# Moving tensor_tensor work from GpSimd to VectorE, deeper buffers in the first norm, and float32r parts for the modulation products

## The chip, the cores and the metric

The kernel runs on one core of a Trainium2 chip. The metric is the device time of one execution in microseconds (us). The median of three runs of the kernel before is 2357.48 us (2355.71 to 2359.46).

## The reference

One inference step of a two-layer hybrid diffusion model on 640 tokens: 512 latent tokens and 128 context tokens, D = 1024, all float32. Per layer:

```python
mod = silu(c) @ w_mod[l] + b_mod[l]          # 1024 -> 6*1024, for c and for c_ctx
sh1, sc1, g1, sh2, sc2, g2 = split(mod, 6)
h = rmsnorm(x, g_pre_mix) * (1 + sc1) + sh1
z = h @ w_in                                  # one projection for three mixers and the gates
oa, ob, oc = windowed_gqa(z), latent_attention(z), qknorm_gqa(z)
m = sum(sigmoid(gate_i) * (o_i @ w_oi)) @ w_out
x = x + g1 * rmsnorm(m, g_post_mix)
h = rmsnorm(x, g_pre_mlp) * (1 + sc2) + sh2
x = x + g2 * rmsnorm(square(relu(h @ w_mlp1)) @ w_mlp2, g_post_mlp)
```

The new keys and values of the context tokens are outputs too.

## The kernel before

**Products.** A float32 matrix product is made from float32r parts: each operand is split into a high part (ScalarE copies it into a float32r tile) and a low part (VectorE subtracts the high part from the source), and three products hi*hi, hi*lo, lo*hi are added up in PSUM (`mm3`, L574). `unit` (L540) loads a weight block into a `wr` buffer and splits it into `wh` and `wl`; these come from a ring of `NW` = 4 buffers. The modulation is the exception: there TensorE takes plain float32 operands.

**Stages.** `run` (L1913) goes through `first_norm` (RMSNorm of the five 128-token tiles, transposes, and the first two modulation vectors of layer 0), then per layer: `b_proj`, `b_rope`, `b_heads` (latent attention), the two GQA mixers in four groups (`gqa_group`), `merge`, `wout` with `post` and `norm_mod` after each token tile, `mlp1_first`, `sums` and 14 rounds of `mlp1_pair` (one Strassen-Winograd level: seven products for two column blocks of the MLP; the weights are first combined into s1 to s4), and `mlp2_block`. Gates (`gate_gen`) and modulation (`mod_gen`) are fillers: `drive` advances them at given rates while attention or MLP runs.

**Order.** All instructions are first recorded by `Recorder` (L168) and then ordered per engine by a list scheduler: `one` (L386) simulates engines with the costs of `cost`, `latest` (L361) computes the latest finishing time of each instruction, which becomes its rank on VectorE, ScalarE, GpSimd and SyncE in the next of 8 passes; the best pass is emitted (L528, so nearly all rows of the profile have line L528). In `one` a transfer holds the network for its bytes / 300e3 us. The scheduler also knows that a GpSimd tensor_tensor and a VectorE instruction with operands in SBUF alone lengthen each other.

**What the change touches.** `first_norm` (L823): the token tiles `x0` have 3 buffers, the 1 MB weight blocks `mw` 4 (`[P, 4, 512]`, eight blocks in all); a float32 matmul has the 128x2 condition vectors `scT` as its stationary operand and gives a 2x512 row, which ScalarE copies (`modrow`) and four small transposes turn into columns (`modt`). The first projection (`b_proj`, 288 columns) runs in two halves, k = 0 to 3 and k = 4 to 7, since the normed inputs `hh`/`hl` of k = 4 to 7 need the second half of these vectors. `mod_gen` (L715): two accumulators of 128x512, one for each condition vector, take eight weight rows per half vector; the first is accumulated by VectorE (`scalar_tensor_tensor`), the second by a ScalarE scaling and a GpSimd add. The sum over partitions is a float32 matmul against ones: for gates (v = 2, 5) 128x512 outputs, otherwise eight products with one column. GpSimd also adds in `rope` (called from `kv_evac`, `q_evac`, `b_rope`), in `prompt_group`, `merge`, `post` (token tiles 0 and 1) and `mlp1_pair` (s1 to s4, name `s` in the profile). Its normalisation of probabilities (`normalise`, L987, tile `pt`) and the `pow` of the norms (`rs`, `hrs`) are not touched.

Of the kernel before, what the change touches and what calls it, by code (L numbers as in the profile page):

```python
# [11 lines left out]
F32 = mybir.dt.float32  # L12
F32R = mybir.dt.float32r
# [4 lines left out]
P = 128  # L18
# [149 lines left out]
class Recorder:  # L168
# [192 lines left out]
    def latest(self, everything, end):  # L361
# [10 lines left out]
        for o in reversed(self.done):  # L372
            for p, data in o.preds.items():
                t = o.late
                if data:
                    t -= p.end - p.start
                    if o.eng is not None and p.eng != o.eng:
                        t -= self.LAT
# [7 lines left out]
    def one(self, everything, look):  # L386
# [49 lines left out]
        while True:  # L436
# [32 lines left out]
            if o.dma:  # L469
                net = max(net, t + 1.6) + wait / 300e3  # L470
# [61 lines left out]
class Step:  # L532
# [70 lines left out]
    def setup(self, ctx):  # L603
# [36 lines left out]
        self.scT = c.tile([P, 2, 8], F32, name="scT")  # L640
        self.modT = [c.tile([P, 6, 8, 2], F32, name=f"modT{l}") for l in range(DEPTH)]
# [23 lines left out]
    def cond(self):  # L665
# [9 lines left out]
        nc.vector.tensor_tensor(self.scT.rearrange("p s k -> p (s k)"), cT, r, ALU.mult)  # L675
        for l in range(DEPTH):
# [38 lines left out]
    def mod_gen(self, mp, l, vecs, own=0):  # L715
# [3 lines left out]
        for v in vecs:  # L719
            for hf in range(2):  # L720
                c0 = v * D + hf * 512
                acc = [mp.tile([P, 512], F32, name=f"macc{s}", tag=f"macc{s}", bufs=1) for s in range(2)]
                for u in range(4):
# [6 lines left out]
                    for j in range(2):  # L730
# [5 lines left out]
                        else:  # L736
                            nc.vector.scalar_tensor_tensor(out=acc[0], in0=rv[:, j, :], scalar=s0, in1=acc[0],
                                                           op0=ALU.mult, op1=ALU.add)
                            nc.scalar.activation(rv[:, j, :], rv[:, j, :], AF.Copy, scale=s1)
                            nc.gpsimd.tensor_tensor(acc[1], acc[1], rv[:, j, :], ALU.add)  # L740
                    yield
                isg = v in (2, 5)
                if isg:
# [5 lines left out]
                    for s in range(2):  # L749
                        ps = self.bank("mps", "pt")  # L750
                        nc.tensor.matmul(ps, self.ones, acc[s], start=True, stop=True)
# [4 lines left out]
                else:  # L756
                    ps = self.bank("mps", "pt")
                    pv = ps[:, :8].rearrange("p (n s) -> p n s", s=2)
                    for n in range(4):
                        for s in range(2):  # L760
                            nc.tensor.matmul(pv[:, n, s:s + 1], acc[s][:, n * P:n * P + P], self.ones[:, 0:1], start=True, stop=True)
# [61 lines left out]
    def first_norm(self, pool, xin):  # L823
# [3 lines left out]
        xs = [pool.tile([P, D], F32, name="x0", tag="x0", bufs=3) for t in range(NT)]  # L827
# [15 lines left out]
        for n in range(2):  # L843
            if n == 1:
                self.first = self.proj_units(I["w_in"][0], 768 + 384, 288, 3)
            for v in (1, 0):
                ps = self.lin_ps()
                for kh in range(2):
                    raw = pool.tile([P, 4, 512], F32, name="mw", tag="mw", bufs=4)
                    nc.sync.dma_start(raw, self.wsrc(w, 4 * kh, 4, v * D + n * 512, 512))  # L850
                    for i in range(4):
                        k = 4 * kh + i
                        nc.tensor.matmul(ps[:2, :], self.scT[:, :, k], raw[:, i], start=k == 0, stop=k == KC - 1)
                row = pool.tile([2, 512], F32, name="modrow", tag="modrow", bufs=2)
                nc.scalar.activation(row, ps[:2, :], AF.Copy)
                tps = self.bank("modt", "pt")
                pv = tps[:, :8].rearrange("p (n s) -> p n s", s=2)
# [1298 lines left out]
```

## Time and profile before

| | |
|---|---|
| median of 3 runs | 2357.48 us |
| profiled execution, its own time | 2356.36 us |
| its span | 2354.6 us |
| PE busy | 2286.6 us, 97% |
| PEld busy (weight loads, beside PE) | 2089.6 us, 89% |
| DVE (VectorE) busy | 1700.6 us, 72% |
| ACT (ScalarE) busy | 1289.2 us, 55% |
| POOL (GpSimd) busy | 763.2 us, 32% |
| DMA | 317.10 MB, 135 GB/s |

PE is TensorE. A matmul's record covers its pass through the array, so consecutive records overlap; what a matmul costs in a dense stretch is the distance from its start to the start of the next one. A float32 matmul shows as two records.

### The profile page before, as it was taken

Reading aid. Unit: us, or ns where it says so; the run is one execution under the profiler, and the core shown is the slowest. Engines: PE = TensorE matmul, PEld = TensorE weight load, DVE = VectorE, ACT = ScalarE, POOL = GpSimd, SP = SyncE. Lnnn points to the kernel's source line nnn. Section 1 sums busy time; section 2 is a strip of 40 time slices with the busy share of each in tenths; the row PEclk is TensorE's granted clock in tenths of the full one; section 3 lists DMA queues with packets and bytes.
Section 4 is the critical chain, followed back from the end, with each engine's and each line's share of the span. In section 5 each row is a group of like instructions: output and inputs, shape, how many; then the busy total and the mean of one; then the engine's idle time right before and its main releaser. Section 6 shows DMA issues by size and latency. Waiting matters only on the chain. (4 is left out here: it accounts for less than half of the span.)

```text
span 2354.6 us, 39546 instructions
## 1 busy us (share of the span) xinstructions
PE 2286.6 (97%) x14303; PEld 2089.6 (89%) x14303; DVE 1700.6 (72%) x3351; ACT 1289.2 (55%) x3000; POOL 763.2 (32%) x671
## 2 busy tenths in 40 slices
PE   8999999999999999999999999999999999999998
PEld 3988999989998999888889889899999889998886
DVE  3778488897675998867477866998846669884444
ACT  4577466676435565744265765767743356664222
POOL 1322044562132475223033212455412315650001
PEclk9999999999999999999999999999999999999999
DMA  7431244343663454664244222434346544446332
GB/s 252 112 91 50 86 121 129 104 107 96 218 208 113 149 170 146 224 209 150 80 134 113 65 82 75 127 105 125 109 152 187 177 135 150 165 139 215 117 120 81
DMA packets 252451, 317.10 MB, mean 135 GB/s; under 512 B 37328, under 2 KB 169696, under 8 KB 251744
## 3 DMA queue, kind: packets, MB, share of 16 engines
q1 hardware_dynamic: 252256, 314.58, 42.9%
q8 instruction: 113, 1.85, 0.3%
q14 instruction: 82, 0.67, 0.1%
HBM read 251.84 MB, written 57.44 MB: 131 GB/s over the span
## 5 line engine op out<-in xcount | busy, mean ns | idle before, releaser
L528 DVE TENSOR_TENSOR wl<-wr,wh 128x256 fp32r<-128x256 f32 (+5 forms) x772 | 370.5, 527 | 145.0 <-ACT wh L528 143.6
L528 ACT ACTIVATE wh<-wr 128x256 fp32r<-128x256 f32 (+5 forms) x772 | 276.2, 421 | 257.5 <-PE lps L528 140.0
L528 POOL TENSOR_SCALAR pt<-pt,rc 128x640 f32<-128x640 f32 (+1 forms) x192 | 167.4, 879 | 315.3 <-DVE rc L528 261.2
L528 PE MATMUL lps<-wh,ah 128*128 128x512 f32 x640 | 252.8, 395 | 0.0
L528 PE MATMUL lps<-wh,al 128*128 128x512 f32 x640 | 252.4, 394 | 0.0
L528 PE MATMUL lps<-wl,ah 128*128 128x512 f32 x640 | 251.9, 394 | 0.0
L528 POOL TENSOR_TENSOR rs<-ss,mhalf 128x1 f32<-128x1 f32 x60 | 37.1, 619 | 497.5 <-DVE ss L528 496.6
L528 DVE TENSOR_TENSOR pl<-tps,ph 128x512 fp32r<-128x512 f32 (+2 forms) x240 | 147.8, 631 | 30.3 <-ACT ph L528 27.6
L528 ACT ACTIVATE pt<-sps,nm 128x640 f32<-128x640 f32 (+2 forms) x192 | 141.7, 741 | 50.9 <-DVE nm L528 48.6
L528 PE MATMUL sps<-h2h,wl 128*128 128x320 f32 (+2 forms) x464 | 145.0, 313 | 9.8 <-DVE wl L528 9.8
L528 ACT ACTIVATE ph<-tps 128x512 fp32r<-128x512 f32 (+2 forms) x240 | 130.4, 555 | 33.0 <-PE tps L528 29.9
L528 PE MATMUL sps<-h2h,wh 128*128 128x320 f32 (+2 forms) x464 | 145.9, 314 | 0.0
L528 PE MATMUL tps<-ident,pt 128*128 128x128 f32 x896 | 140.5, 275 | 5.2 <-POOL pt L528 1.9
L528 PEld LDWEIGHTS lps<-wl,ah 128*128 128x128 f32 x640 | 120.1, 188 | 28.5 <-issue 0.2
L528 PEld LDWEIGHTS lps<-wh,ah 128*128 128x128 f32 x640 | 120.1, 188 | 28.0 <-issue 0.5
L528 PE MATMUL sps<-h2l,wh 128*128 128x320 f32 (+2 forms) x464 | 144.6, 312 | 0.0
L528 PEld LDWEIGHTS lps<-wh,al 128*128 128x128 f32 x640 | 120.1, 188 | 27.5
L528 POOL TENSOR_TENSOR macc<-macc,wr 128x512 f32<-128x512 f32 x84 | 118.3, 1409 | 57.2 <-ACT wr L528 44.4
L528 POOL TENSOR_TENSOR s<-wq 128x512 f32<-128x512 f32 x56 | 89.8, 1604 | 142.4 <-DMA wq<-in_w_mlp 116.9
L528 POOL TENSOR_TENSOR macc<-macc,mr 128x512 f32<-128x512 f32 x56 | 87.7, 1566 | 140.5 <-ACT mr L528 92.9
L528 DVE TENSOR_TENSOR wl<-s,wh 128x512 fp32r<-128x512 f32 x112 | 123.3, 1114 | 3.4 <-ACT wh L528 2.2
L528 PE MATMUL gps<-hh,wh 128*128 128x320 f32 x384 | 120.1, 313 | 2.2 <-ACT th L528 1.7
(335 smaller groups left out, 7371.4 us busy)
## 6 DMA issues: line engine op xcount, KB each, us to landing
wr<-in_w_in SPq DMA_DIRECT2D x72, 512.0 KB, 3.8
wr<-in_w_mlp SPq DMA_DIRECT2D x72, 512.0 KB, 4.0
wq<-in_w_mlp SPq DMA_DIRECT2D x56, 512.0 KB, 4.1
wr<-in_w_mod SPq DMA_DIRECT2D x48, 512.0 KB, 3.8
ar<-a SPq DMA_DIRECT2D x56, 320.0 KB, 4.5
mr<-in_w_mod SPq DMA_DIRECT2D x32, 512.0 KB, 4.6
th<-th SPq DMA_DIRECT2D x96, 160.0 KB, 1.9
tg<-th SPq DMA_DIRECT2D x48, 320.0 KB, 3.1
```

What stands on the lines that cost most here:

```text
L528: getattr(getattr(self.nc, o.eng), o.name)(*args, **kw)
```

## The change

Every GpSimd `tensor_tensor` over full tiles becomes a VectorE one; in `mod_gen` the scaling and the add become one VectorE `scalar_tensor_tensor`. Both accumulators are then split into float32r parts and multiplied with float32r ones, or with a 128x2 selector `pick` whose 2x512 result is copied and transposed as in the first norm. In `first_norm` the weights are split on chip into `wh`/`wl`, the condition vectors into four columns `scs` (two high, two low), so one float32 matmul becomes two float32r ones with four columns; `x0` has 5 buffers, `mw` 8, and the weights of the first projection are recorded after the norm instead of inside it. In the scheduler a transfer now counts as 370e3 bytes per us, and the latest time of what feeds a transfer's reader is taken from that.

```diff
@@ latest / one
-                    t -= p.end - p.start
+                    t -= 2.3 + p.wait / 370e3 if p.dma else p.end - p.start
-                net = max(net, t + 1.6) + wait / 300e3
+                net = max(net, t + 1.6) + wait / 370e3
@@ cond
+        for i in range(2):
+            nc.vector.tensor_copy(self.scs[:, :, i], self.scT[:, i, :])
+            nc.vector.tensor_tensor(self.scs[:, :, 2 + i], self.scT[:, i, :], self.scs[:, :, i].bitcast(F32), ALU.subtract)
@@ mod_gen
-                            nc.scalar.activation(rv[:, j, :], rv[:, j, :], AF.Copy, scale=s1)
-                            nc.gpsimd.tensor_tensor(acc[1], acc[1], rv[:, j, :], ALU.add)
+                            nc.vector.scalar_tensor_tensor(out=acc[1], in0=rv[:, j, :], scalar=s1, in1=acc[1],
+                                                           op0=ALU.mult, op1=ALU.add)
+                hi = self.ws.tile([P, 1024], F32R, name="wh", tag="wh", bufs=self.NW)
+                lw = self.ws.tile([P, 1024], F32R, name="wl", tag="wl", bufs=self.NW)
+                parts = [(hi[:, s * 512:s * 512 + 512], lw[:, s * 512:s * 512 + 512]) for s in range(2)]
+                for s, (ah, al) in enumerate(parts):
+                    nc.scalar.activation(ah, acc[s], AF.Copy)
+                    nc.vector.tensor_tensor(al, acc[s], ah.bitcast(F32), ALU.subtract)
-                        nc.tensor.matmul(ps, self.ones, acc[s], start=True, stop=True)
+                        nc.tensor.matmul(ps, self.onesr, parts[s][0], start=True, stop=False)
+                        nc.tensor.matmul(ps, self.onesr, parts[s][1], start=False, stop=True)
+                    for s in range(2):
+                        for i in range(2):
+                            nc.tensor.matmul(ps[:2, :], self.pick[:, 1 - s:3 - s], parts[s][i], start=s + i == 0, stop=s + i == 2)
+                    row = acc[0][:2, :]
+                    nc.scalar.activation(row, ps[:2, :], AF.Copy)
+                    ps = self.bank("modt", "pt")
                     for n in range(4):
-                        for s in range(2):
-                            nc.tensor.matmul(pv[:, n, s:s + 1], acc[s][:, n * P:n * P + P], self.ones[:, 0:1], start=True, stop=True)
+                        nc.tensor.transpose(pv[:, n, :], row[:, n * P:n * P + P], self.ident[:2, :2])
@@ first_norm
-        xs = [pool.tile([P, D], F32, name="x0", tag="x0", bufs=3) for t in range(NT)]
+        xs = [pool.tile([P, D], F32, name="x0", tag="x0", bufs=5) for t in range(NT)]
-            if n == 1:
-                self.first = self.proj_units(I["w_in"][0], 768 + 384, 288, 3)
-                    raw = pool.tile([P, 4, 512], F32, name="mw", tag="mw", bufs=4)
+                    raw = pool.tile([P, 4, 512], F32, name="mw", tag="mw", bufs=8)
-                        nc.tensor.matmul(ps[:2, :], self.scT[:, :, k], raw[:, i], start=k == 0, stop=k == KC - 1)
+                        nc.scalar.activation(wh, raw[:, i], AF.Copy)
+                        nc.vector.tensor_tensor(wl, raw[:, i], wh.bitcast(F32), ALU.subtract)
+                        nc.tensor.matmul(ps[:4, :], self.scs[:, k, :], wh, start=k == 0, stop=False)
+                        nc.tensor.matmul(ps[:4, :], self.scs[:, k, :], wl, start=False, stop=k == KC - 1)
+        self.first = self.proj_units(I["w_in"][0], 768 + 384, 288, 3)
@@ prompt_group, kv_evac, q_evac, b_rope, merge, post, mlp1_pair: the same in each
-                        nc.gpsimd.tensor_tensor(m, m, th, ALU.add)
+                        nc.vector.tensor_tensor(m, m, th, ALU.add)
-        tt = nc.gpsimd.tensor_tensor
+        tt = nc.vector.tensor_tensor
```

Counted over the program, VectorE has 3353 instructions before and 3792 now, POOL 676 and 320, ACT 2719 and 2663; TensorE has 14209 matmuls and transposes before and 14161 now.

How the order moves, at three places. First, SyncE's queue at the start of the program (`mw` are the eight weight blocks of the modulation, `x0` the token tiles, `wr` weights of the projection). Before:

```order
L528 DMA mw_115<-in_w_mod 128x4x512
L528 DMA wr_105<-in_b_mod 48x128
L528 DMA sinB_126<-in_k_sinB 128x4x32
L528 DMA wr_133<-in_w_in 128x3x288
L528 DMA wr_137<-in_w_in 128x3x288
L528 DMA cosB_143<-in_k_cosB 128x4x32
L528 DMA x0_155<-in_x_sample 128x1024
```

and now:

```order
L528 DMA x0_113<-in_x_sample 128x1024
L528 DMA mw_115<-in_w_mod 128x4x512
L528 DMA x0_117<-in_x_sample 128x1024
L528 DMA x0_125<-in_x_prompt 128x1024
L528 DMA mw_131<-in_w_mod 128x4x512
L528 DMA mw_140<-in_w_mod 128x4x512
L528 DMA mw_145<-in_w_mod 128x4x512
L528 DMA mw_152<-in_w_mod 128x4x512
L528 DMA mw_163<-in_w_mod 128x4x512
L528 DMA mw_171<-in_w_mod 128x4x512
L528 DMA mw_175<-in_w_mod 128x4x512
L528 DMA wr_181<-in_w_in 128x3x288
```

Before, four blocks go out, then two weight blocks of the projection, and the last two token tiles and the other four blocks wait for buffers. Now all five token tiles and all eight blocks stand ahead of the projection's weights, and none waits for a buffer.

Second, TensorE where the modulation of layer 0 is summed inside the attention groups (`macc` are the accumulators, `tps`, `ops` and `gps` attention and gate work). Before, the first three of a group of eight:

```order
L528 MATMUL gps<-hl,wh 128x320
L528 MATMUL gps<-hh,wl 128x320
L528 MATMUL mps<-ones,macc_4645 128x1
L528 MATMUL mps<-ones,macc_4687 128x1
L528 MATMUL mps<-ones,macc_4645 128x1
```

and now:

```order
L528 MATMUL gps<-hh,wl 128x320
L528 MATMUL mps<-wh,pick 2x512
L528 MATMUL mps<-wl,pick 2x512
L528 MATMUL mps<-wh,pick 2x512
L528 MATMUL mps<-wl,pick 2x512
L528 MATMUL tps<-ident,pt 128x128 x3
L528 MATMUL ops<-ph,V 128x512
L528 MATMUL ops<-pl,V 128x512
L528 MATMUL ops<-ph,V 128x256
L528 MATMUL ops<-pl,V 128x256
L528 MATMUL modt<-ident,macc_4804 128x2 x4
```

Eight one-column products become four products with two rows, and seven attention instructions stand between them and the four transposes that need ScalarE's copy.

Third, VectorE where the MLP's Strassen rounds of layer 0 begin (`t0l` to `t3l` are low parts of sums of the normed input, `wq` the raw weights, `s12` and `s34` their combinations). Before:

```order
L528 TENSOR_TENSOR t2l_9782<-hfull_9239,t2h_9757 128x640
L528 TENSOR_TENSOR t0l_9813<-hfull_9239,t0h_9785 128x640 x2
L528 TENSOR_TENSOR wl_9833<-wq_9752,wh_9816 128x512
L528 TENSOR_TENSOR hfull_9239<-hfull_9239 128x2x320
L528 TENSOR_TENSOR wl_9833<-wq_9752,wh_9816 128x512
L528 TENSOR_TENSOR wl_9884<-s12_9839,wh_9872 128x512
```

and now:

```order
L528 TENSOR_TENSOR t2l_9930<-hfull_9387,t2h_9905 128x640
L528 TENSOR_TENSOR s34_9963<-wq_9900 128x512
L528 TENSOR_TENSOR wl_9970<-wq_9900,wh_9958 128x512
L528 TENSOR_TENSOR s12_9979<-wq_9900 128x512
L528 TENSOR_TENSOR wl_9970<-wq_9900,wh_9958 128x512
L528 TENSOR_TENSOR s12_9979<-s12_9979,wq_9900 128x512
L528 TENSOR_TENSOR wl_10004<-s34_9963,wh_9984 128x512
L528 TENSOR_TENSOR t0l_10012<-hfull_9387,t0h_9933 128x640
```

The weight combinations stand among the splits, and the two low parts of the first weights come ahead of `t0l`.

## Rows read from the trace of the kernel before

**Rows 1.** The page: span, and busy time of each engine.

```profile
span 2354.6 us, 39546 instructions
PE 2286.6 (97%) x14303; PEld 2089.6 (89%) x14303; DVE 1700.6 (72%) x3351; ACT 1289.2 (55%) x3000; POOL 763.2 (32%) x671
```

**Rows 2.** Busy time by stretch: start, attention of layer 0, Strassen rounds of both layers.

```profile
core 0: us, PE busy (x) PEld busy (x) DVE busy (x) ACT busy (x) POOL busy (x), PEclk, DMA share, GB/s
30.00:35.00 5.00, 4.10 (x18) 2.06 (x18) 0.14 (x1) 1.20 (x2) 0.84 (x1) 0.66 1.06 388
60.00:600.00 540.00, 522.49 (x3708) 495.52 (x3707) 426.64 (x970) 342.58 (x858) 191.99 (x203) 1.00 0.35 100
789.00:963.00 174.00, 174.00 (x1169) 173.04 (x1170) 156.33 (x221) 109.51 (x195) 104.37 (x65) 0.99 0.47 156
```

**Rows 3.** Waits of PE over the program: us in total, times, longest.

```profile
PE sps L528 <- DVE wl L528: 9.8, 2, 5.1
PE ops L528 <- DVE pl L528: 6.5, 12, 1.5
```

**Rows 4.** Timeline of PE, 30 to 58 us: start, us, instructions.

```profile
30.90 1.62 PE L528 MATMUL nps<-ident,xn 128*128 128x128 f32 x8 [2.83 <-POOL xn L528]
...
47.29 3.60 PE L528 MATMUL lps<-mw,scT 128*2 128x512 f32 x8
...
51.94 0.41 PE L528 MATMUL modt<-ident,modrow 2*128 2x2 f32 x4
...
55.68 0.29 PE L528 MATMUL lps<-wh,hh 128*128 128x288 f32 x1
...
57.27 0.29 PE L528 MATMUL sps<-wh,hh 128*128 128x288 f32 x1
```

**Rows 5.** The chain that ended last: output product, MLP start and modulation of layer 1.

```profile
1875.03 11.07 PE fps L528 x48
...
1937.57 1.90 DVE t0l L528
1939.47 1.67 DVE wl L528
1941.14 1.80 DVE hfull L528
...
2069.99 1.72 PE mps L528 x4
```

**Rows 6.** Timeline of SP's queue, ACT and DVE in the first 60 us.

```profile
28.06 0.59 SPq L528 DMA_DIRECT2D mw<-in_w_mod x1
...
4.32 1.06 ACT L528 ACTIVATE xn<-x 128x1024 f32<-128x1024 f32 x1 [2.32 <-DMA x<-in_x_sample]
...
28.61 1.05 ACT L528 ACTIVATE hf<-nps 128x512 f32<-128x512 f32 x2
...
21.98 2.15 DVE L528 TENSOR_TENSOR wl<-wr,wh 128x432 fp32r<-128x432 f32 x4
```

**Rows 7.** Timeline of PE at 421 us: a one-column sum of the modulation.

```profile
421.18 1.84 PE L528 MATMUL mps<-ones,macc 128*128 128x1 f32 x16
422.88 0.53 PE L528 MATMUL tps<-ident,pt 128*128 128x128 f32 x3
```

**Rows 8.** Groups of DVE by form, whole program: count, busy us, mean ns, idle before.

```profile
L528 DVE TENSOR_TENSOR wl<-wr,wh 128x256 fp32r<-128x256 f32 x696 | 323.7, 514 | 142.2 <-ACT wh L528 141.3 <-DMA wr<-in_w_mlp 0.2
L528 DVE TENSOR_TENSOR wl<-s,wh 128x512 fp32r<-128x512 f32 x112 | 123.3, 1114 | 3.4 <-ACT wh L528 2.2
L528 DVE TENSOR_TENSOR pl<-tps,ph 128x512 fp32r<-128x512 f32 x176 | 117.9, 685 | 29.0 <-ACT ph L528 26.5
```

**Rows 9.** The same view for 2200 to 2320 us alone.

```profile
L528 DVE TENSOR_TENSOR wl<-wr,wh 128x256 fp32r<-128x256 f32 x72 | 26.1, 419 | 40.5 <-ACT wh L528 40.5
```

**Rows 10.** Tiles `macc` and `pt`: ns min/median/max, first and last start, forms.

```profile
L528 DVE SCALAR_TENSOR_TENSOR macc<-wr,scT,macc x84: 722/750/1862, 93.0 to 1666.9; 128x512 f32<-128x512 f32 x84
...
L528 POOL TENSOR_SCALAR pt<-pt,rc x192: 577/803/1871, 131.6 to 1724.6; 128x640 f32<-128x640 f32 x128, 128x384 f32<-128x384 f32 x32, 128x512 f32<-128x512 f32 x32
```

More of the change, by code (lines that the diff above doesn't have):

```diff
@@ L640, in setup @@
         self.scT = c.tile([P, 2, 8], F32, name="scT")
+        self.scs = c.tile([P, 8, 4], F32R, name="scs")
+        self.pick = c.tile([P, 3], F32R, name="pick")
+        pick = self.sm.tile([P, 3], F32, name="pick32")
+        nc.vector.memset(pick, 0.0)
+        nc.vector.memset(pick[:, 1:2], 1.0)
+        nc.vector.tensor_copy(self.pick, pick)
         self.modT = [c.tile([P, 6, 8, 2], F32, name=f"modT{l}") for l in range(DEPTH)]
@@ L852, in first_norm @@
                         k = 4 * kh + i
-                        nc.tensor.matmul(ps[:2, :], self.scT[:, :, k], raw[:, i], start=k == 0, stop=k == KC - 1)
-                row = pool.tile([2, 512], F32, name="modrow", tag="modrow", bufs=2)
-                nc.scalar.activation(row, ps[:2, :], AF.Copy)
+                        if i % 2 == 0:
+                            hi = self.ws.tile([P, 1024], F32R, name="wh", tag="wh", bufs=self.NW)
+                            lw = self.ws.tile([P, 1024], F32R, name="wl", tag="wl", bufs=self.NW)
+                        wh, wl = (t[:, i % 2 * 512:i % 2 * 512 + 512] for t in (hi, lw))
+                        nc.scalar.activation(wh, raw[:, i], AF.Copy)
+                        nc.vector.tensor_tensor(wl, raw[:, i], wh.bitcast(F32), ALU.subtract)
+                        nc.tensor.matmul(ps[:4, :], self.scs[:, k, :], wh, start=k == 0, stop=False)
+                        nc.tensor.matmul(ps[:4, :], self.scs[:, k, :], wl, start=False, stop=k == KC - 1)
+                row = pool.tile([4, 512], F32, name="modrow", tag="modrow", bufs=2)
+                nc.scalar.activation(row, ps[:4, :], AF.Copy)
                 tps = self.bank("modt", "pt")
-                pv = tps[:, :8].rearrange("p (n s) -> p n s", s=2)
+                pv = tps[:, :16].rearrange("p (n s) -> p n s", s=4)
                 for j in range(4):
-                    nc.tensor.transpose(pv[:, j, :], row[:, j * P:j * P + P], self.ident[:2, :2])
+                    nc.tensor.transpose(pv[:, j, :], row[:, j * P:j * P + P], self.ident[:4, :4])
                 ks = slice(4 * n, 4 * n + 4)
-                nc.vector.tensor_tensor(mod[:, v, ks], pv, self.vecT[0][:, 8 * v:8 * v + 8][:, ks].unsqueeze(2).to_broadcast([P, 4, 2]), ALU.add)
+                nc.vector.tensor_tensor(mod[:, v, ks], pv[:, :, 0:2], self.vecT[0][:, 8 * v:8 * v + 8][:, ks].unsqueeze(2).to_broadcast([P, 4, 2]), ALU.add)
+                nc.vector.tensor_tensor(mod[:, v, ks], pv[:, :, 2:4], mod[:, v, ks], ALU.add)
                 if v:
@@ L1165, in prompt_group @@
         nc.vector.reciprocal(den, den)
-        nc.gpsimd.tensor_tensor(p3, p3, den.unsqueeze(2).to_broadcast([P, 4, P]), ALU.mult)
+        nc.vector.tensor_tensor(p3, p3, den.unsqueeze(2).to_broadcast([P, 4, P]), ALU.mult)
         yield
@@ L1212, in turn @@
                     cs = (self.cosA, self.sinA) if isA else (self.cosK, self.sinK)
-                    res["k"] = self.rope(pool, k, 2, cs[0][:, t], cs[1][:, t], 16, nc.gpsimd)
+                    res["k"] = self.rope(pool, k, 2, cs[0][:, t], cs[1][:, t], 16, nc.vector)
                     self.put_v(V, t, v)
@@ L1248, in turn @@
                     cs = (self.cosA, self.sinA) if isA else (self.cosQ, self.sinQ)
-                    res["q"] = self.rope(pool, q, 4, cs[0][:, t], cs[1][:, t], 16, nc.gpsimd)
+                    res["q"] = self.rope(pool, q, 4, cs[0][:, t], cs[1][:, t], 16, nc.vector)
                 elif isA:
@@ L1426, in b_rope @@
             if t < 4:
-                r = self.rope(pool, pv, 8, self.cosB[:, t], self.sinB[:, t], 8, nc.gpsimd)
+                r = self.rope(pool, pv, 8, self.cosB[:, t], self.sinB[:, t], 8, nc.vector)
                 nc.scalar.activation(self.qr[:, t], r, AF.Copy)
@@ L1693, in post @@
             nc.vector.scalar_tensor_tensor(out=f[:, c], in0=src[:, c], scalar=r, in1=self.gg[:, s, c], op0=ALU.mult, op1=ALU.mult)
-            (nc.vector if t >= 2 else nc.gpsimd).tensor_tensor(x[:, c], x[:, c], f[:, c], ALU.add)
+            nc.vector.tensor_tensor(x[:, c], x[:, c], f[:, c], ALU.add)
             nc.sync.dma_start(out[:, c], x[:, c])
```

## The prediction, made before the change was run

> **What bounds the kernel now.** I read the page first: TensorE is busy 97% of the span, VectorE 72% and POOL 32% [rows 1]. So the time is TensorE's work plus what TensorE waits for. The stretches say where waits can lie: in the Strassen rounds TensorE is busy throughout, while attention of layer 0 leaves 540.00 - 522.49 = 17.5 us of 540 open, and VectorE is busy 426.64 us there [rows 2]. The table of TensorE's waits gives the largest: 9.8 us in two waits for `wl`, where the Strassen rounds of the two layers begin, then 6.5 us for `pl` [rows 3]. What can shorten the kernel is therefore less work on TensorE, an earlier start of its dense part, and shorter waits on VectorE's results. POOL's 763.2 us count only where somebody waits for them or is slowed by them.
>
> The sum below is made against the profiled execution (2356.36 us, 1.76 us above its span); that one is 1.12 us below the median. A difference of 0.2%, 4.7 us, is about what a measurement of this kernel can tell from none.
>
> **The start: -11 us.** The first projection's second half needs the last of the first norm's modulation vectors; its matmuls start at 57.27 us, and from there on TensorE is dense [rows 4]. Before that TensorE works off 32 float32 products; a group of eight records, four products, takes 3.60 us, 0.9 us each [rows 4], some 28 us. Afterwards they are 64 float32r products at the pitch of the dense output product, 11.07 / 48 = 0.231 us [rows 5]: 14.8 us. TensorE no longer sets this stage, so I take the latest of three others. Transfers: five token tiles of 0.52 MB and eight blocks of 1.05 MB are 11.0 MB, at the 388 GB/s that the trace shows with the queue full [rows 2] 28.4 us, from about 2 us on, so about 30.5; before, the last block was issued only at 28.06 us, after a buffer had come free [rows 6]. VectorE: 32 splits at 2.15 / 4 x 512 / 432 = 0.64 us [rows 6] are 20.4 us, done by 31 if they follow the blocks. ScalarE: from 4.32 us five squares of some 1.2 us, ten copies, 32 splits and three row copies at 1.05 / 2 = 0.53 us [rows 6] make 6 + 45 x 0.53 = 30 us, so about 35. ScalarE is last. The first half of the projection, 60 matmuls at (57.27 - 55.68) / 12 = 0.1325 us [rows 4], then takes until about 44; ScalarE and VectorE need about as long for the remaining scaling and splits of `hh`, `hl` and weights. The second half starts at about 45 to 46 instead of 57.27: -11 to -12. I take -11. Best case, ScalarE hidden and transfers last: -15. Worst case: TensorE's records show the clock at a mean of 0.66 of full speed in the slice after an idle 2.83 us [rows 2, 4]; if the sparse products ran at 1.2 GHz throughout, 64 x 0.46 us and then 60 x 0.265 us put the second half at about 54, -3.
>
> **Modulation sums: -6.4 and -4.4 us.** A gate half vector takes four records, 1.72 us [rows 5]; four float32r products at 0.231 us take 0.92. Eight of them: -6.4 us. The other half vectors took 16 records from 421.18 to 422.88, 1.70 us [rows 7]; now four float32r products, 0.92 us, and four small transposes, 0.41 us [rows 4], together 1.33. Twelve of them: -4.4 us. These stand in TensorE's queue amid dense work, so they come off the end almost whole (bounds -6 to -6.4 and -3.5 to -5). The new ScalarE copy between products and transposes, under 0.6 us, is covered by the attention instructions that now stand there.
>
> **Starts of the Strassen rounds: -7 us.** Here VectorE's chain runs into GpSimd's adds: `t0l` 1.90 us, `wl` 1.67, `hfull` 1.80 [rows 5], where a 128x512 subtraction with one input in PSUM keeps 0.685 us over the whole program [rows 8]. Moving s1 to s4 to VectorE costs it four instructions a round, but ends this company, and the new order puts two combinations and the two first splits ahead of `t0l`: four instructions, some 2.7 us, after the last `t1l`/`t2l`, instead of `t0l` twice, `wl`, `hfull` and `wl`, about 8.8 us. TensorE waited 5.1 and 4.7 us [rows 3]; I take 3.5 off each. Bounds: 0, if the products behind wait as long, and -9.8, the whole row.
>
> **VectorE's load: -2 us.** Given back is what GpSimd's adds cost VectorE: `wl<-s` takes 1114 ns against those 685 [rows 8], 112 x 0.43 = 48 us; a 128x256 split 514 over the program and 419 in a late stretch with little POOL work [rows 8, 9], 696 x 0.095 = 66 us; the accumulations, which spread from 722 to 1862 ns [rows 10], and the other splits some 60 by the same ratio. About 175 us. Added, by durations: 140 accumulations at 0.750 us [rows 10], 112 combinations and 72 splits of 128x512 at 0.685 [rows 8], and smaller adds (56 of the rotations, 32 of the merge, 16 others) of some 60 us by their size: about 290 us. VectorE would end near 1700 + 290 - 175 = 1815 us, 77 to 78% of the shorter span.
>
> The Trainium skill's page SBUF — State Buffer, section Who interferes with whom, has it that a VectorE instruction with two SBUF inputs and a GpSimd instruction that reads SBUF exclude each other for their whole length. The trace agrees in kind, as `pl` with an input in PSUM is spared; but by the rule the 192 normalisations that stay on POOL, 803 ns in the median, could hold VectorE for up to 154 us, this term would then go to its bad end, +12, and the sum below to -17.
>
> Does VectorE become the bound? A Strassen round takes TensorE 174 / 14 = 12.4 us and VectorE 156.33 / 14 = 11.2 [rows 2]. Four combinations at 0.685 and half a filler's two accumulations add 3.5 us, the four `wl<-s` give back 1.7 and the other splits about 1: 12 of 12.4, close but below. Attention of a layer gains 42 accumulations, 31 us, and some 20 us of splits and rotations, against 540 - 426.64 = 113 us idle [rows 2], before anything is given back. I book shorter waits for `pl` against longer queues: -2, bounds -10 (the 6.5 us for `pl` [rows 3] and some others) and +12 (half a us in each Strassen round less what the starts of the rounds leave). ScalarE loses 140 scalings and gains 72 splits and 12 rows; it stays near 55%, and neither of TensorE's largest waits is for it.
>
> **Sum.** -11 - 6.4 - 4.4 - 7 - 2 = -30.8. 2356.4 - 30.8 = 2325.6, plus 1.1 to the median: 2327 us. Its own range: all terms at the good end give -46, 2311; at the bad end -0.5, 2357; 2314 to 2345 is what I hold likely for this case.
>
> **Rivals.**
> *The start gains nothing* (16%). The clock stays low and ScalarE, now with 32 splits more, runs late. For it: ScalarE's 30 us leave no slack, and the slice at 0.66 [rows 2]. Against: TensorE had 28 us of float32 work there. -30.8 + 11 = -20: 2338.
> *Normalisations and VectorE block each other; slower* (8%). POOL's 192 normalisations stay, each between an exponential and TensorE's transposes, and their durations already spread from 577 to 1871 ns [rows 10]. VectorE now has some 300 more instructions with two SBUF inputs. If each normalisation waits for one of them, 0.69 us, that is 132 us of latency. It decides from 31 / 132, a quarter, reaching TensorE; at a half it is 66 - 31 = +35: 2392. Against: the spread comes at least in part from GpSimd's own adds queued in between, and TensorE's largest waits are for `wl` and `pl`, not for `pt` [rows 3]. The same section of the Trainium skill speaks for this rival, as the lock holds for GpSimd's tensor_scalar too; no row here separates it.
> *Attention's waits fall as well* (13%). Without GpSimd's adds VectorE's queue has no instruction of over 1 us in front of `pl` but reductions; 15 us more go: 2312.
> *The change doesn't do what it says for the time* (6%). The scheduler now counts on 370 GB/s; if transfers come later than planned, by 0.1 us for each of the some 300 weight blocks, TensorE waits 30 us and the gain is gone: 2357. For it: nothing in the rows shows such rates while results are written back too. Against: 388 GB/s [rows 2].
>
> **How the numbers follow.** 57% for the forecast, 2327 us. Faster by over 0.2% holds for it, the first and the third rival: 0.86. Within 0.2%: 0.06, the fourth. Slower: 0.08. The range takes in the third rival, the first, and most of the bad end of the forecast: 2309 to 2350.
>
> **What would show each step.** Float32 products of `lps` and `mps` gone; the second half of the projection starting at 44 to 47 us; waits of `sps` on `wl` under 4 us in all; `wl<-s` at about 0.69 us and the 128x256 splits at about 0.42; VectorE near 77%, POOL near 11%. I am wrong if the projection starts after 52 us, if TensorE's waits on DVE or POOL exceed those of before by over 15 us, or if a row of waits on DMA appears.

## The result, and the profile after

Four runs of the changed kernel took 2333.69 us in the median (2332.34 to 2335.18), the kernel before, on the same chip, 2357.09 us (2355.71 to 2359.46). The ratio is 0.990, with a 95% interval from 0.9883 to 0.9917: 23.4 us faster. 2327 was forecast, with a range of 2309 to 2350. The page of the changed kernel, beside [rows 1]:

```profile
span 2330.5 us, 39134 instructions
...
PE 2267.8 (97%) x14207; PEld 2072.6 (89%) x14207; DVE 1747.5 (75%) x3790; ACT 1247.0 (54%) x2944; POOL 263.3 (11%) x315
```

TensorE is busy 18.8 us less and bounds the kernel as before. The spans differ by 24.0 us. The table cuts the two spans at the same matmuls, found in the timelines of PE: `sps<-ckh,wh` is the first product of latent attention, `fps` that of the output projection, `lps<-wh,ah` that of the MLP's second half.

| stage, us | before | change | difference |
|---|---|---|---|
| start to latent attention of layer 0 | 118.0 | 111.3 | -6.6 |
| to the output projection (attention, o-products) | 578.3 | 579.4 | +1.1 |
| to the MLP's second half (Strassen rounds) | 268.2 | 261.1 | -7.1 |
| to latent attention of layer 1 | 308.9 | 306.6 | -2.2 |
| to the output projection | 578.4 | 577.4 | -1.0 |
| to the MLP's second half | 269.1 | 261.2 | -7.9 |
| to the end | 233.7 | 233.5 | -0.3 |

So the gain lies at the start and in the two stages with Strassen rounds; both attentions are as long as they were. The table of TensorE's waits, whose first two rows before were [rows 3], has no wait of `sps` for `wl` any more, and the largest is now the one for the rows of the condition vectors at the start:

```profile
PE rowps L528 <- DMA wr<-in_c_ctx: 6.6, 1, 6.6
PE sps L528 <- DVE qd L528: 4.3, 6, 0.8
PE sps L528 <- ACT pt L528: 4.2, 9, 1.1
PE ops L528 <- DVE pl L528: 4.1, 12, 0.7
...
PE tps L528 <- POOL pt L528: 3.6, 7, 0.7
```

The stretches of [rows 2], of the changed kernel:

```profile
core 0: us, PE busy (x) PEld busy (x) DVE busy (x) ACT busy (x) POOL busy (x), PEclk, DMA share, GB/s
...
60.00:600.00 540.00, 518.87 (x3650) 488.99 (x3649) 433.69 (x1042) 326.96 (x828) 109.40 (x126) 1.00 0.36 104
...
789.00:963.00 174.00, 174.00 (x1158) 171.61 (x1157) 160.96 (x296) 106.68 (x188) 0.00 (x0) 1.00 0.51 166
```

POOL is empty in the Strassen rounds, and VectorE has only 4.6 us more to do there, although it took over four combinations a round. The groups of DVE by form show why (compare [rows 8]):

```profile
L528 DVE TENSOR_TENSOR wl<-wr,wh 128x256 fp32r<-128x256 f32 x696 | 265.1, 430 | 138.6 <-ACT wh L528 137.7
...
L528 DVE TENSOR_TENSOR pl<-tps,ph 128x512 fp32r<-128x512 f32 x176 | 118.0, 684 | 29.3 <-ACT ph L528 27.1
...
L528 DVE TENSOR_TENSOR wl<-s,wh 128x512 fp32r<-128x512 f32 x112 | 74.5, 684 | 3.6 <-ACT wh L528 3.3
```

The low parts of `s` fell from 1114 to 684 ns, the 128x256 splits from 514 to 430; `pl`, which reads PSUM, kept its 684. VectorE has 439 records more than before and only 47 us more busy time.

**The Strassen starts.** In the kernel before, the timeline of PE shows the wait, and what came behind it:

```profile
783.92 0.31 PE L528 MATMUL sps<-h2l,wh 128*128 128x320 f32 x1
788.89 0.51 PE L528 MATMUL sps<-h2h,wl 128*128 128x320 f32 x1 [4.67 <-DVE wl L528]
789.20 0.47 PE L528 MATMUL sps<-h2h,wh 128*128 128x320 f32 x1
...
792.13 0.47 PE L528 MATMUL sps<-h2h,wl 128*128 128x320 f32 x1
...
792.58 0.31 PE L528 MATMUL sps<-h2l,wh 128*128 128x320 f32 x1
```

and the busy time of the same stretches, also before:

```profile
784.00:789.00 5.00, 0.34 (x3) 0.11 (x2) 5.00 (x4) 1.80 (x4) 4.92 (x4) 1.00 0.00 0
789.00:792.40 3.40, 3.40 (x14) 3.40 (x15) 3.40 (x3) 3.40 (x9) 3.40 (x3) 0.51 0.11 39
```

Behind the wait of 4.67 us the granted clock is 0.51 (the 1.2 GHz level) up to 792.4, and a product of 320 columns comes every 0.267 us instead of every 0.147. Thirteen of them cost 1.6 us on top of the wait; in layer 1 the same comes to some 2.3 us behind a wait of 5.12. Neither is there in the changed kernel; the two stages are 7.1 and 7.9 us shorter. VectorE's chain shows why. The low parts `t0l`, before and in the change:

```profile
L528 DVE TENSOR_TENSOR t0l<-hfull,t0h 128x640 fp32r<-128x640 f32 x4 | 7.5, 1914 | 0.0
L528 DVE TENSOR_TENSOR t0l<-hfull,t0h 128x640 fp32r<-128x640 f32 x4 | 3.3, 816 | 0.0
```

Behind the last `t2l` of layer 0, `t0l` twice, `wl`, `hfull` and `wl` took 8.9 us up to 788.8 us; now two combinations and two `wl` take 2.5 us, up to 777.2.

**The start.** The queue of SP and the bytes moved in each us from 0 to 40, of the changed kernel:

```profile
3.41 0.32 SPq L528 DMA_DIRECT2D wr<-in_b_mod  x1
4.66 0.27 SPq L528 DMA_DIRECT2D wr<-in_g_pre_mix  x1
6.12 0.27 SPq L528 DMA_DIRECT2D wr<-in_g_pre_mlp  x1
6.44 0.36 SPq L528 DMA_DIRECT2D x<-in_x_sample  x1
6.84 0.43 SPq L528 DMA_DIRECT2D mw<-in_w_mod  x1
```

```profile
GB/s 0 16 168 406 409 120 0 78 279 387 406 412 434 401 393 391 385 387 389 385 387 389 379 391 389 385 389 381 391 389 383 389 393 371 349 349 325 233 155 28
```

Two small rows wait in SP's queue until 4.66 and 6.12 us, and the blocks behind them go out only then (the first at 6.84 us, at 3.42 before): between 5 and 8 us next to nothing moves. What they wait for is not a buffer. They are the ninth and tenth transfer of the queue, and the trace has them take over the semaphores of the first two, token tiles, when those have landed:

```profile
SPq L528 <- DMA x<-in_x_sample: 2.1, 2, 1.2
```

The last block is there at 35.7 us, as ACT shows, and TensorE's products of the first norm end at 39.8:

```profile
35.71 1.68 ACT L528 ACTIVATE wh<-mw 128x512 fp32r<-128x512 f32 x3 [0.54 <-DMA mw<-in_w_mod]
```

```profile
39.41 0.39 PE L528 MATMUL lps<-wl,scs 128*4 128x512 f32 x1
39.75 0.53 PE L528 MATMUL sps<-wh,hh 128*128 128x288 f32 x2
...
49.06 0.29 PE L528 MATMUL sps<-wh,hh 128*128 128x288 f32 x1
```

Before, the projection began at 44.97 us, with eight records of float32 products (3.5 us) still among its matmuls [rows 4]; 5.2 and 3.5 are 8.7 us. Its sixty-first product, the first of the second half, starts at 49.06 us, where the prediction gave 44 to 47 as its sign: 8.2 us earlier than the 57.27 of before. The last product is 7.0 us earlier, behind a new wait of `bps` of 1.0 us at 57.2, and 6.6 us reach latent attention.

**The sums.** A gate sum before and in the change, then a two-row sum in the change:

```profile
2069.83 1.88 PE L528 MATMUL mps<-macc,ones 128*128 128x512 f32 x4
2071.14 0.71 PE L528 MATMUL sps<-h2h,wh 128*128 128x320 f32 x1
2071.69 0.31 PE L528 MATMUL sps<-h2l,wh 128*128 128x320 f32 x1
```

```profile
2046.86 0.39 PE L528 MATMUL mps<-wh,onesr 128*128 128x512 f32 x1
...
2047.76 0.31 PE L528 MATMUL sps<-h2h,wh 128*128 128x320 f32 x1
2047.91 0.31 PE L528 MATMUL sps<-h2l,wh 128*128 128x320 f32 x1
```

```profile
413.23 0.40 PE L528 MATMUL mps<-wh,pick 128*2 128x512 f32 x1
...
414.16 0.49 PE L528 MATMUL tps<-ident,pt 128*128 128x128 f32 x3
...
415.27 0.41 PE L528 MATMUL modt<-ident,macc 2*128 2x2 f32 x4
415.61 0.55 PE L528 MATMUL tps<-ident,pt 128*128 128x128 f32 x3
```

Up to the product behind it the gate sum takes 1.31 us before and 0.90 now; but before, that product's successor starts 0.55 us later and not 0.15. With that delay it is 1.71 against 0.90. The other sum takes 1.70 [rows 7] and 0.1 behind it before, now 0.93 + 0.34 and some 0.2 around the transposes. From start to start alone all sums take TensorE 31.9 us before and 24.1 after (the expectations below count so); with the delays behind them the difference is about 10 us.

### The profile page after: what moved, and what is told of

Read it like the earlier page. It is cut to its first block, busy times and chain, and to the rows that moved or that the text cites. A ratio compares the mean times of both kernels' runs of the same rounds, so it can differ in the third digit from the quotient of the medians.

```text
span 2330.5 us, 39134 instructions
## 1 busy us (share of the span) xinstructions
PE 2267.8 (97%) x14207; PEld 2072.6 (89%) x14207; DVE 1747.5 (75%) x3790; ACT 1247.0 (54%) x2944; POOL 263.3 (11%) x315
## 5 line engine op out<-in xcount | busy, mean ns | idle before, releaser
L528 DVE TENSOR_TENSOR wl<-wr,wh 128x256 fp32r<-128x256 f32 (+5 forms) x772 | 305.8, 443 | 142.0 <-ACT wh L528 140.8
L528 POOL TENSOR_SCALAR pt<-pt,rc 128x640 f32<-128x640 f32 (+1 forms) x192 | 174.9, 920 | 627.7 <-DVE rc L528 569.4
L528 ACT ACTIVATE pt<-sps,nm 128x640 f32<-128x640 f32 (+1 forms) x192 | 142.0, 741 | 55.7 <-DVE nm L528 41.1
L528 DVE SCALAR_TENSOR_TENSOR macc<-wr,scT,macc 128x512 f32<-128x512 f32 x168 | 126.3, 776 | 3.6 <-DMA wr<-in_w_mod 2.2
L528 PEld LDWEIGHTS tps<-ident,pt 128*128 128x128 f32 x896 | 106.4, 140 | 18.2 <-POOL pt L528 6.4
L528 PE MATMUL sps<-oh,wh 128*128 128x320 f32 x384 | 118.9, 310 | 0.8 <-ACT oh L528 0.7
L528 PE MATMUL gps<-hh,wl 128*128 128x320 f32 x384 | 119.6, 311 | 0.0
```

The lines of the kernel that those rows point to most:

```text
L528: getattr(getattr(self.nc, o.eng), o.name)(*args, **kw)
```

## The experiments

Theory after these traces: each part's gain stands where it shows, start 6.6, sums 7.8 to 10, Strassen starts 13 to 14, less some waits. Rival: the parts need each other, or the scheduler's new order makes them. First each part alone, against the kernel before (2359.5 us on the chips of these runs), then each part taken back out of the whole change.

**First norm alone** (with the float32r condition vectors):

```diff
-        xs = [pool.tile([P, D], F32, name="x0", tag="x0", bufs=3) for t in range(NT)]
+        xs = [pool.tile([P, D], F32, name="x0", tag="x0", bufs=5) for t in range(NT)]
...
-                    raw = pool.tile([P, 4, 512], F32, name="mw", tag="mw", bufs=4)
+                    raw = pool.tile([P, 4, 512], F32, name="mw", tag="mw", bufs=8)
...
-                        nc.tensor.matmul(ps[:2, :], self.scT[:, :, k], raw[:, i], start=k == 0, stop=k == KC - 1)
+                        nc.tensor.matmul(ps[:4, :], self.scs[:, k, :], wh, start=k == 0, stop=False)
+                        nc.tensor.matmul(ps[:4, :], self.scs[:, k, :], wl, start=False, stop=k == KC - 1)
```

> The kernel before with the changed first norm alone (five token tiles, eight weight blocks, float32r parts and four condition columns, projection weights recorded after the norm). In the trace of the whole change the first attention product of the prompt starts 6.6 us earlier than before. Theory: that is the first norm's own work, so alone it gives 5.5 to 7 us, about 2351. Rival: it needs the faster VectorE of the other parts or the other transfer rates; then 0 to 3 us, about 2355, with the first projection starting after 43 us instead of 39.75.

2362.4 us, ratio 1.0013 (1.0004 to 1.0022): slower. Its timeline of PE begins with

```profile
14.54 0.25 PE L528 MATMUL rowps<-ident,wr 16*128 16x16 f32 x1 [14.54 <-DMA wr<-in_c_ctx]
...
17.20 0.59 PE L528 MATMUL lps<-wh,scs 128*4 128x512 f32 x1 [1.70 <-DVE scs L528]
```

With nothing to wait for a buffer, the old transfer figures put two blocks and four token tiles ahead of 4 KB that everything needs. The theory falls, and the part's worth hangs on the order. The late rows themselves are not the loss: latent attention starts at 118.2 us, 0.3 later than before. The profiled execution (2367.0 us) loses in attention of layer 0, 585.9 us instead of 578.3, where three stretches at half the clock, from 126.6, 505.5 and 611.3 us, are new.

**Sums alone** (splits, products and transposes of `mod_gen`; scaling and add as before):

```diff
-                        nc.tensor.matmul(ps, self.ones, acc[s], start=True, stop=True)
+                        nc.tensor.matmul(ps, self.onesr, parts[s][0], start=True, stop=False)
+                        nc.tensor.matmul(ps, self.onesr, parts[s][1], start=False, stop=True)
...
-                            nc.tensor.matmul(pv[:, n, s:s + 1], acc[s][:, n * P:n * P + P], self.ones[:, 0:1], start=True, stop=True)
+                        nc.tensor.transpose(pv[:, n, :], row[:, n * P:n * P + P], self.ident[:2, :2])
```

> The kernel before with the float32r modulation sums alone (splits, gate products, two-row products and transposes; the scaling on ScalarE and the add on GpSimd stay). Theory: in the two traces the sums take TensorE 31.9 us from start to start before and 24.1 after, 7.8 us less, and TensorE is dense around them, so 6 to 8 us, about 2350. Rival: the added copy and splits make TensorE wait as long as the products save, 0 to 2 us, about 2356.

2357.4 us, 0.9989 (0.9981 to 0.9997): 2.1 us. TensorE's sums take 23.8 us as expected, but its waits grew (`kps` for `kst` 6.2 us instead of 2.5, `gps` for `pz` 3.1 instead of 1.6), and three stretches at half the clock are new (from 492, 608 and 1540 us). The rival holds.

**Strassen combinations alone:**

```diff
-        tt = nc.gpsimd.tensor_tensor
+        tt = nc.vector.tensor_tensor
```

> The kernel before with one line changed: the combinations s1 to s4 of the MLP's Strassen rounds on VectorE instead of GpSimd. Theory: the company of GpSimd's adds at the start of the rounds caused both waits of 4.7 to 5.1 us and the 3.2 us at half the clock behind each; both go, 12 to 14 us, about 2344, and the low parts of s take 0.69 instead of 1.11 us. Rival 1: the waits go only with the new order that the other transfer rates give, 0 to 4 us, about 2355. Rival 2: VectorE becomes late inside the rounds or in attention, no gain or slower, 2357 or more.

2344.9 us, 0.9940 (0.9926 to 0.9954): 14.6 us with one line, as the theory says. The two stages take 261.7 and 261.5 us, as in the whole change; the low parts of `s` take 735 ns.

**Transfer figures alone:**

```diff
-                    t -= p.end - p.start
+                    t -= 2.3 + p.wait / 370e3 if p.dma else p.end - p.start
...
-                net = max(net, t + 1.6) + wait / 300e3
+                net = max(net, t + 1.6) + wait / 370e3
```

> The kernel before with the scheduler's two new transfer figures alone. Theory: no work changes and TensorE has no wait on transfers of weights in the trace, so within 3 us of before, 2354 to 2360, and the waits where the Strassen rounds begin stay at 4 to 5 us each. Rival: the new order by itself ends those waits, 8 us or more faster, under 2349.

2360.9 us, 1.0005 (0.9995 to 1.0016): no difference. Half of the expectation on the waits was wrong: they fell to 4.9 us in three, the longest 2.0. The gain is lost elsewhere: latent attention starts at 122.6 us, 4.6 later than before, and TensorE has new waits for `ah` of 2.8 and 1.7 us where the MLP's second halves begin.

**First norm and figures together** (the diffs of the first and the fourth run):

> The kernel before with the changed first norm and the scheduler's two new transfer figures together, neither of which gave anything alone. In the first run the rows of the condition vectors went out behind 4 MB of blocks and tokens, and TensorE waited 14.5 us for them instead of 6.2; with the new figures the order has them third and fourth again. Theory: the start is a joint work of the two, so together 5 to 8 us faster than before, and the first attention product of the prompt starts near 111 to 113 us. Rival: the start also needs a VectorE freed of GpSimd's adds; then 0 to 3 us, and the first projection still starts after 43 us.

2356.0 us, 0.9982 (0.9971 to 0.9993). The condition vectors are early again (6.4 us), the projection starts at 40.02 us, but latent attention only at 115.4, 2.6 us earlier than before. Between the two: the pair makes the start, and some 4 us of it come only with the rest of the change.

**Both figures back** (the fourth run's diff undone in the whole change):

> The whole change with the scheduler's two old transfer figures. The order again has two blocks and four token tiles ahead of the condition vectors. Theory: the start's gain is lost and turns into a loss as in the first run, 7 to 11 us slower than the whole change, 2341 to 2345 where the change has 2334, with the wait for the condition vectors at 13 us or more; the Strassen rounds stay without a wait. Rival: with the other parts in place the figures do not matter, within 3 us.

2329.8 us, 0.9879 (0.9865 to 0.9892): 3.9 us faster than the whole change, though the intervals still touch. The start does get late (14.6 us of wait, latent attention at 117.9, as late as in the kernel before), and all of it is made up by the output projection of layer 0: attention takes 572.7 us, against 579.4. Neither had foreseen it.

**Combinations back on GpSimd** (the third run's diff undone):

> The whole change with the combinations s1 to s4 back on GpSimd. Theory: the waits where the two Strassen rounds begin return with the time at half the clock behind them, 10 to 14 us slower than the whole change, 2344 to 2348 where that has 2334; TensorE waits 4 us or more twice there. Rival: the waits needed the rest of GpSimd's work as well, or the other order, and only 0 to 5 us return.

2341.2 us, 7.5 us slower than the whole change. Both stages take 264.5 us, 3.4 more. The first waits of the MLP in this run:

```profile
783.70 0.41 PE L528 MATMUL sps<-h2h,wl 128*128 128x320 f32 x1 [1.62 <-DVE wl L528]
783.95 0.31 PE L528 MATMUL sps<-h2h,wh 128*128 128x320 f32 x1
...
788.77 0.42 PE L528 MATMUL sps<-t1h,wl 128*128 128x320 f32 x1 [1.29 <-DVE wl L528]
789.02 0.31 PE L528 MATMUL sps<-t1h,wh 128*128 128x320 f32 x1
```

Instead of one wait of 4.67 us there are shorter ones, and behind them the products keep the full pace (granted clock 1.00). So the order decides whether GpSimd's company costs 3.4 or 7 us a stage here; with the combinations on VectorE no run has a wait of over 0.3 us for these `wl`.

**Sums back to float32** (the second run's diff undone):

> The whole change with the modulation sums in float32 again (the scaled adds stay on VectorE). Theory: in the whole change VectorE and ScalarE have room for the splits, so the products' 7.8 us come back almost whole: 5 to 8 us slower than the whole change, 2339 to 2342. Rival: as alone, the splits and the copy cost as much in attention as the products save: within 3 us, or even faster.

2336.4 us, 2.7 us slower: nearer to the rival. TensorE's sums take 33.4 us from start to start, 9.2 more, and 10 with the delays. 3.5 us of that come back where one does not look for them, in the dense products of layer 0's MLP (see the last section). The 2.7 us are not the price of the sums alone: in the new order latent attention starts 4.6 us later than in the whole change, and attention of layer 0 is 3.2 us shorter.

**One figure back:**

```diff
-                net = max(net, t + 1.6) + wait / 370e3
+                net = max(net, t + 1.6) + wait / 300e3
```

> The whole change with only one of the two transfer figures old again (300e3 bytes per us in the running estimate; the latest times keep the new figure). TensorE's order from the first attention group on is then nearly that of the run with both figures old, and the condition vectors go out third and fourth as in the whole change. In that run the first attention product stood 6.6 us later than in the whole change, and the first output product at the same time. Theory (taken up): attention of layer 0 is paced by other engines than TensorE and takes up what the start gives, so the time is within 2 us of that run, 2328 to 2332. Rival (carried through): it was the better order of attention that caught up there, and the earlier start comes on top, 4 to 7 us less, 2323 to 2326.

2326.1 us, 0.9861 (0.9847 to 0.9874), under the whole change's interval. Latent attention at 114.3 us, attention 571.9 and 574.3 us. 3.7 us less than with both figures back, whose latent attention came 3.6 us later: the start is carried through.

**First norm back** (the first run's diff undone):

> The whole change with the first norm as before (float32 products, three token and four weight buffers). Theory (taken up): TensorE's dense part starts 5 to 7 us later and attention takes that up; within 3 us of the whole change, 2331 to 2337. Rival (carried through): all of it shows at the end, 5 to 8 us slower, 2339 to 2342.

2341.9 us, 8.2 us slower: most of it is carried through. But the start itself is 11.5 us later, not 5 to 7 (latent attention at 122.8 us), as the new figures delay the old first norm here as they did alone (122.6); attention of layer 0 takes up 2.8.

**The other moves back on GpSimd** (the same in `kv_evac`, `q_evac`, `b_rope`, `merge`, `post`, `prompt_group`):

```diff
-                            nc.vector.scalar_tensor_tensor(out=acc[1], in0=rv[:, j, :], scalar=s1, in1=acc[1],
-                                                           op0=ALU.mult, op1=ALU.add)
+                            nc.scalar.activation(rv[:, j, :], rv[:, j, :], AF.Copy, scale=s1)
+                            nc.gpsimd.tensor_tensor(acc[1], acc[1], rv[:, j, :], ALU.add)
```

> The whole change with the rotations, the merge, the residual adds, the prompt's normalisation and the second modulation accumulation back on GpSimd (its scaling on ScalarE); the Strassen combinations stay on VectorE. Theory: GpSimd's adds then slow VectorE again, the 128x256 splits beside one to some 1.0 us from 0.42, and TensorE waits longer for parts of attention, 2 to 6 us slower than the whole change, 2336 to 2340. Rival 1: VectorE gains as much room as it loses, within 2 us. Rival 2: what VectorE took over in attention holds TensorE up, so 2 to 6 us faster, 2328 to 2332.

2342.7 us, 9.0 us slower, more than the theory had. 4.7 us are at the start, 1.8 between the MLP's second half and latent attention of layer 1, 2.2 in its attention; the 77 splits of 128x256 beside an add alone take 1043 ns on average, those beside nothing 418.

**The start ordered as in the change, the rest as with one figure back:**

```diff
-                net = max(net, t + 1.6) + wait / 370e3
+                net = max(net, t + 1.6) + wait / (370e3 if t < 60 else 300e3)
```

> The whole change with the running estimate of transfers at the new figure in the first 60 us of the plan and at the old one behind: the start is ordered as in the whole change, everything from the second attention stage on nearly as in the run with the figure old throughout (2326.1 us), whose first attention product stood 3.0 us later than in the whole change. Theory (carried through): both gains add, 2.0 to 4.0 us less than that run, 2322 to 2324, and the rest of the gap to the whole change (2333.7) lies in the two attentions and what follows them. Rival (taken up): the 3 us are lost in attention of layer 0 again, within 1.5 us of that run, 2325 to 2327.5.

2324.5 us, 0.9850 (0.9836 to 0.9864). Latent attention stands at 112.4 us, 1.9 earlier than with one figure back; the span is 1.7 shorter. The median falls between the two expectations, because the start gained less than the 3.0 us counted on; what it gained was carried. This is the fastest of all, 9.2 us under the whole change by the medians:

```profile
span 2320.4 us, 39117 instructions
...
60.00:600.00 540.00, 522.50 (x3688) 493.61 (x3687) 433.89 (x1046) 328.91 (x833) 111.33 (x127) 1.00 0.36 106
```

In these 540 us TensorE stands still 3.6 us less than in the whole change, and VectorE works as long. No single wait explains it: over the whole program those for `pt`, `kst`, `oraw` and `pl` are each 0.4 to 1.4 us shorter.

| part | alone, us | in the whole change, by medians | by the ratios to before |
|---|---|---|---|
| Strassen combinations | -14.6 | -7.5 | -6.1 |
| other moves off GpSimd | not run | -9.0 | -8.7 |
| first norm | +2.9 | -8.2 | -7.3 |
| sums | -2.1 | -2.7 | -1.2 |
| transfer figures | +1.4 | +3.9 | +5.0 |

The whole change was timed apart from the others, and the kernel before stood 2 us higher in theirs; the last column multiplies the difference of the ratios by 2357. The parts add up to -23.5 by the medians and -18.3 by the ratios, against -23.4. Every one of these kernels is ordered anew, so a figure holds what the order did as well; 2 to 3 us of each should not be leaned on. That the medians add up to the whole is then partly chance. The first norm and the figures cannot be told apart here: the -8.2 holds the delay that the new figures give the old norm, with both figures old the new norm starts latent attention no earlier than before (117.9 and 118.0 us), and the whole change with the old norm and the old figures was not run.

One thing runs through all of these: how long TensorE's clock stood at its lower level. Summed from the clock's records without the end of the program, it is 17.1 us before, 3.4 in the whole change, none with one figure back, but 30.7 with the first norm alone, 27.3 with the sums alone and 13.7 with the sums back. Where TensorE is busy throughout, half of such time is lost (an estimate from the pace above, 0.267 instead of 0.147 us).

## Why the prediction was right, and where not

The direction, the engine that bounds and, but for the sums, the places of the gain were right, the total 6.7 us too low. That it came so near is in part luck: the sums were put some 8 to 10 us too high and the start 3 to 4, the starts of the Strassen rounds 6 us too low, and the term for VectorE hides two larger ones. By its steps:

- **The start, -11.** Mis-sized: -8.2 at the second half of the projection, -6.6 at latent attention. The step that failed is "so about 30.5" for the transfers: the last block came at 35.7 us. Two small rows held SP's queue, and the engines moved almost nothing for 3 us, worth 2.5 us at 388 GB/s; and 11.8 MB had passed by then, not 11.0, worth 2 us. ScalarE, which I took for last, ended its splits only behind that block (38.4 us). That the start hangs on the scheduler's figures was not seen: alone, without them, this part made the kernel 2.9 us slower, and in the change with both old the start is not early at all.
- **Modulation sums, -6.4 and -4.4.** As TensorE's time both were about right: eight times 1.71 against 0.93 is -6.2, and twelve times 1.8 against 1.47 about -4, of which a wait of 1.3 us inside one sum takes a third. What failed is "they come off the end almost whole": 10 us less TensorE time were worth 1 to 3, alone and in the whole change. In the whole change 3.5 go into the slower pace of the products behind, in layer 0. Alone the pace gives no loss over the two layers; there TensorE's waits grew from 57.6 to 63.1 us in all, and its time at half the clock by 10.2 us. That the 40 splits each that ScalarE and VectorE now make more are behind those waits was not tested.
- **Starts of the Strassen rounds, -7, bounds 0 and -9.8.** The mechanism was right, the bound wrong: "the whole row" is the wait alone, and the time at half the clock behind it, 1.6 and 2.3 us of loss, was not priced. -7.1 and -7.9 with 0.8 us each from a gate sum: some -13.4; alone, without the sums, -14.1.
- **VectorE's load, -2.** Two larger things cancelled here: the other moves are worth 9.0 us and the new running figure takes back 7.6 (2333.7 against 2326.1 us). VectorE ended at 1747 us, not 1815: by the durations some 300 us were added and some 215 came back, 40 more than booked, and its records overlap by 227 us instead of 190, which the busy time counts once.
- **The rivals.** Normalisations blocking VectorE did not come:

```profile
L528 POOL TENSOR_SCALAR pt<-pt,rc x192: 583/807/2974, 125.0 to 1709.7; 128x640 f32<-128x640 f32 x128, 128x384 f32<-128x384 f32 x32, 128x512 f32<-128x512 f32 x32
```

The median is 807 ns against 803 [rows 10], five of the 192 take over 1.5 us instead of one, and TensorE waits 3.6 us for `pt` instead of 1.9. The 66 splits of 128x256 beside a normalisation take 556 ns on average (median 415), the others 417: 9 us of VectorE's time, where the prediction's bound was 154 for all its instructions. The rule in the Trainium skill's page SBUF — State Buffer, section Who interferes with whom, thus holds in kind (GpSimd's reads lengthen a two-input VectorE instruction) and is far from its worst case here. "Attention's waits fall as well" did not come in the change, but does in part with the old running figure. The fourth rival was right that the figure costs something, but TensorE itself waits for no transfer: no row of its waits in attention names a DMA. ScalarE does: in attention of layer 0 it waits 10.9 us for `orw` in the change and 5.8 with one figure back, but TensorE's waits for the `oh` made from it differ by only 0.3 us. So it looks like the order of the other work; why just this order is worse stays open, and the runs with the old figure share one order of attention, so that 300 is the better number in general is not shown.

## What to carry to other kernels

Price a wait on TensorE with what follows it: a wait of some us is paid a second time if the granted clock falls. TensorE time saved is not time saved: here 10 us of it gave 1 to 3, while one line that ended two waits gave 7 to 14. Where a scheduler orders everything, a buffer or a rate changes the order far away: test each part both alone and taken out, and look at which small load stands behind the big ones.

## What the runs showed of the hardware

The dense 128x512 float32r products of the MLP's second half run at one of two paces in most runs, 0.229 or 0.2333 us. Before, in layer 0, ahead of the sum at 1022 us and behind it:

```profile
999.97 0.40 PE L528 MATMUL lps<-wl,ah 128*128 128x512 f32 x1
1000.21 0.40 PE L528 MATMUL lps<-wh,al 128*128 128x512 f32 x1
...
1099.88 0.39 PE L528 MATMUL lps<-wl,ah 128*128 128x512 f32 x1
1100.11 0.39 PE L528 MATMUL lps<-wh,al 128*128 128x512 f32 x1
```

On average 0.2333 us ahead and 0.2290 behind, at a granted clock of 1.00 both times. It is not the sum that changes the pace. In every run that has a change of pace it comes behind product 120 or 240 of a layer's 960, where a column half of `mlp2_block` ends (60 products each in a layer's first block, 120 in the next); at 1022 us the two fall together, but in layer 1 of the same run the pace goes from 0.229 to 0.2333 at 2148 us, 14 us ahead of the sum there. In the whole change all 960 of both layers stay at 0.2333, which costs 3.1 us in layer 0 and 0.5 in layer 1 against before. With the sums alone 120 products of layer 0 and 840 of layer 1 run at 0.229. What sets the pace was not tried.

Waits of about the same length are not followed by the same clock. In the whole change two waits near 596 us, 1.2 us in all, are followed by a clock of 0.65:

```profile
598.00:601.00 3.00, 2.97 (x13) 2.70 (x14) 1.73 (x5) 1.07 (x4) 0.00 (x0) 0.65 1.02 385
```

In the fastest run the same place, with waits of 0.9 us, keeps 1.00:

```profile
595.00:598.00 3.00, 3.00 (x22) 3.00 (x22) 1.26 (x4) 0.64 (x3) 0.00 (x0) 1.00 1.04 407
```

This is 1.7 us of the gap between the two.
